# The plain down projection of a feed-forward block's first pair, placed behind the first two products of its second pair

## The chip, the cores and the metric

The kernel runs on one core of one Trainium2 chip. The metric is the device time of one execution in microseconds (us); the kernel before took 2893.24 us, the median of three runs.

## The reference: what is computed

Two layers are applied with the same weights to 256 prompt tokens and 512 sample tokens, 768 rows of width 1024, all in 32-bit floats.

```python
def swiglu_ffn(x, w_gate, w_up, w_down):
    return (jax.nn.silu(x @ w_gate) * (x @ w_up)) @ w_down
...
        for l in range(DEPTH):                     # 2 layers
            x = layer_norm(ALPHA * x + 0.5 * swiglu_ffn(x, ffn1_w_gate[l], ...), ln1_g[l], ln1_b[l])
            mix = hybrid_mixer(x, w_in[l], ...)    # neighbourhood attention and a bidirectional SSD
            x = layer_norm(ALPHA * x + mix, ln2_g[l], ln2_b[l])
            x = layer_norm(ALPHA * x + 0.5 * swiglu_ffn(x, ffn2_w_gate[l], ...), ln3_g[l], ln3_b[l])
```

The hidden width is 2816. So there are four feed-forward blocks, two in each layer. They are called block 1 to block 4 here, in order of time; between blocks 1 and 2, and between 3 and 4, lies a mixer.

## The kernel before

**Number format.** Every matmul operand is kept as a high and a low part (`XH`, `XL`; a weight tile `w` holds both). One 128-row slice of a matrix product is three matmuls: high by high, high by low, low by high. Making a weight's two parts ("splitting" it) is a copy on ACT (L106) and a subtraction on DVE (L107), or for some of them two ACT instructions and an accumulating DMA that GpSimd issues (L102 to L104).

**One block.** The hidden width is cut into 11 pairs of 256 columns. Pair 0 is plain (`plain_pair`, L408): gate and up products of all 768 tokens over all of the width, in two halves m=0 and m=1 of 128 hidden columns each, then `silu` on ACT (L461) and the product on DVE (L465). `put_h` (L435, L437) then splits the result into four tiles: h0 and h1 hold the first 384 tokens of m=0 and m=1, and h2 and h3 the last 384 tokens. Pairs 1 to 10 (`fast_pair`) use Strassen's scheme in Winograd's form: seven products instead of eight for m=0 (gate) and seven for m=1 (up), each of 12 matmuls of 384 columns (L525). Their order is `0, 1, S2, S1, S3, 3, S4`. The products `0` and `1` read `XH` and `XL` as they are. `S2`, `S3` and `3` read the sums of x called T2, T3 and T4, and `S1` reads T1, which overwrites a part of `XH` and `XL`. `sums_of_x` makes these sums once for each block, behind pair 0, on DVE (L507 to L516, L497), GpSimd (L505, L506, L508) and ACT (L496). Products whose name begins with S also need a sum of weights, which DVE makes (L90) before it is split.

**The plain down projection.** `down(0, 1)` multiplies h0 to h3 with the four down weight tiles of pair 0 and adds half of the result to `y`: for each of six token tiles t it takes two PSUM banks (tags B and C, two buffers each), issues 12 matmuls of 512 columns (L619) that alternate between them, and then evicts both with two DVE instructions (L628). In its middle (t == 2) it splits four more weights. The down projections of later pairs are run in pieces between the products of the pair behind them.

**What sets the order.** The program is written in the order pair 0, sums of x, `down(0, 1)`, pair 1 and so on. A scheduler then gives every engine its own list, mostly by that order and by what it takes to be ready first; an engine runs its list strictly in order, and waits at an instruction whose inputs are not there. The raw weights come through a ring of four tiles (`wraw`), loaded on SP's queue; split product weights go through a ring of five places, w0 to w4 (shown as `w_89` to `w_93`), and the down weights of a pair through w5 to w11 (`w_94` to `w_100`).

Of the kernel before, what the change touches and what calls it, by code (L numbers as in the profile page):

```python
# [11 lines left out]
ALU = mybir.AluOpType  # L12
# [3 lines left out]
P = 128  # L16
# [5 lines left out]
NT = T // P  # L22
# [125 lines left out]
def trunk(ctx, tc, x_in, w_gu, w_dn, w_xbc, w_z, w_qk, w_v, w_out, ln_gb, ln_gbc, conv_wb, gmix, smalls, bias, y_out):  # L148
# [265 lines left out]
    def ffn(l, w, i_ln, pend, emit_out, late=()):  # L414
# [113 lines left out]
        def fast_pair(p):  # L528
# [15 lines left out]
                    v_.tensor_mul(sg[:, i, h], sg[:, i, h], src)  # L544

            units_ = down_units(p - 1) if p - 1 in dnw else []
            half = dn_half.get((l, w, p))
            for i, (m, what) in enumerate(PRODUCTS):
                x, b, first = {0: ("B11", 1, True), 1: ("B21", 2, True), "S2": ("T2", 1, False), "S1": ("T1", 3, True),
# [12 lines left out]
                if (m, 3) in banks and (m, "S3") in saved and (m, "d") not in saved:  # L562
                    block(m, 1, hb, saved[m, "S3"], banks[m, 3])
                    saved[m, "d"] = True
                if i >= 1:
                    for _ in range(min(1 if i == 1 else 2, len(units_))):
                        units_.pop(0)()
# [15 lines left out]
        def down_units(p):  # L583
# [18 lines left out]
                    out.append(run)  # L602
            return out

        def down(a, b):
            last = b == NPAIR
            nf = 2 * (b - a)
            units = ws.get(2 * nf)
            post = []
            for t in range(NT):  # L610
                ps = (bank("B"), bank("C"))
                cols = slice(t % 3 * P, (t % 3 + 1) * P)
                for i in range(nf):
                    if i == RESTAT and len(post) > 1:
                        post.pop(0)()
                    hh, hl = (x[:, cols] for x in hs[4 * ((a + i // 2) % 2) + 2 * (t // 3) + i % 2])
                    for wi, (hx, wx) in enumerate(((hh, 0), (hh, 1), (hl, 0))):
                        for n in range(2):
                            t_.matmul(ps[n], hx, units[2 * i + n][wx], start=(i == 0 and wi == 0),  # L619
                                      stop=(i == nf - 1 and wi == 2))  # L620
                if last:
                    post.append(emit_out(t, ps))
                    if t == 2:
                        ws.split(ws.nget + 3)
                    continue
                for n in range(2):
                    sl = y[:, t, n * 512 : (n + 1) * 512]
                    v_.scalar_tensor_tensor(sl, ps[n], 0.5, sl, op0=ALU.mult, op1=ALU.add)  # L628
                if t == 2:
                    ws.split(ws.nget + 3)  # L630
            return post

        plain_pair(0)
        sums_of_x()
        down(0, 1)
        for p in range(1, NPAIR):
            fast_pair(p)
        tp.close()
# [604 lines left out]
```

## Time and profile before

| | us |
|---|---|
| median of three runs | 2893.24 |
| the three runs | 2893.24, 2877.48, 2894.02 |
| the profiled execution | 2896.72 |
| its span, first to last instruction | 2894.8 |
| PE busy / DVE busy / ACT busy in the span | 2837.5 / 2210.1 / 1580.4 |
| mean granted TensorE clock, as a share of 2.4 GHz | 0.988 |

A row of the profile's timeline gives the start of an instruction or of a merged run of them, how long it took, engine, line, operation, output and inputs, the shape, and in brackets how long the engine had been idle before it and what ended that. Matmuls are pipelined: one of 512 columns is listed with 0.39 us, but in a dense stretch the next one starts 0.23 us later. So the distance between starts is what counts.

### The profile page before, as it was taken

Reading aid. Unit: us, or ns where it says so; the run is one execution under the profiler, and the core shown is the slowest. Engines: PE = TensorE matmul, PEld = TensorE weight load, DVE = VectorE, ACT = ScalarE, POOL = GpSimd, SP = SyncE. Lnnn points to the kernel's source line nnn. Section 1 sums busy time; section 2 is a strip of 40 time slices with the busy share of each in tenths; the row PEclk is TensorE's granted clock in tenths of the full one; section 3 lists DMA queues with packets and bytes.
Section 4 is the critical chain, followed back from the end, with each engine's and each line's share of the span. In section 5 each row is a group of like instructions: output and inputs, shape, how many; then the busy total and the mean of one; then the engine's idle time right before and its main releaser. Section 6 shows DMA issues by size and latency. Waiting matters only on the chain.

```text
span 2894.8 us, 41895 instructions
## 1 busy us (share of the span) xinstructions
PE 2837.5 (98%) x15094; PEld 2521.1 (87%) x15094; DVE 2210.1 (76%) x4207; ACT 1580.4 (55%) x3231; POOL 408.5 (14%) x513
## 2 busy tenths in 40 slices
PE   8999999999999999999989999999999999999998
PEld 7999999888777899999879999989886778999997
DVE  7788887768545888888788888877673458888887
ACT  4556564657455456554645555455654564565643
POOL 2112120100001212121131112100000002121210
PEclk9999999999999999999999999999997999999999
DMA  3465563224323255564216565533233232555642
GB/s 119 117 139 127 128 146 103 103 87 142 124 81 130 70 128 129 126 146 95 95 43 139 121 136 128 127 110 122 88 111 116 76 126 71 131 127 128 145 96 88
DMA packets 128880, 330.26 MB, mean 114 GB/s; under 512 B 14816, under 2 KB 27296, under 8 KB 127904
## 3 DMA queue, kind: packets, MB, share of 16 engines
q1 hardware_dynamic: 82592, 243.68, 26.6%
q0 software_dynamic: 46080, 83.91, 16.8%
q8 instruction: 118, 1.93, 0.3%
q14 instruction: 90, 0.74, 0.1%
HBM read 224.67 MB, written 18.97 MB: 84 GB/s over the span
## 4 chain that ended last, share of the span: by engine, by line
PE 86%; DVE 6%; ACT 3%; DMA 2%; issue 2%; POOL 1%; DVEq 0%; SPq 0%; POOLq 0%; ACTq 0%
PE psA L525 37%; PE psB L597 9%; PE psC L597 7%; PE psA L408 5%; PE psA L1120 5%; PE psA L966 5%; PE psB L619 3%; PE psC L619 3%; PE psB L1055 3%; PE psA L773 2%; PE psA L993 2%; PE psC L1084 2%; DMA wraw<-in_w_dn_dram 1%; PE psB L1073 1%; DVE w L107 1%
## 5 line engine op out<-in xcount | busy, mean ns | idle before, releaser
L525 PE MATMUL psA<-XH,w 128*128 128x384 f32 x2560 | 695.9, 338 | 5.0 <-DMA w<-wraw 5.0
L525 PEld LDWEIGHTS psA<-XH,w 128*128 128x128 f32 x2560 | 467.7, 188 | 13.7 <-DMA w<-wraw 6.3
L104 POOL DMA_DIRECT2D w<-wraw x320 | 273.8, 904 | 1246.3 <-ACT w L103 1165.6
L525 PE MATMUL psA<-XL,w 128*128 128x384 f32 x1280 | 432.3, 338 | 0.0
L106 ACT CAST w<-arena 128x512 fp32r<-128x512 f32 x320 | 198.3, 620 | 236.6 <-DVE arena L90 132.9
L600 DVE SCALAR_TENSOR_TENSOR arena<-psB,arena 128x512 f32<-128x512 f32 x384 | 260.4, 685 | 63.6 <-PE psB L597 62.1
L106 ACT CAST w<-wraw 128x512 fp32r<-128x512 f32 (+1 forms) x320 | 193.9, 620 | 161.2 <-PE psA L525 69.4
L102 ACT CAST w<-wraw 128x512 fp32r<-128x512 f32 x320 | 195.2, 619 | 139.6 <-PE psA L525 64.3
L107 DVE TENSOR_TENSOR w<-wraw,w 128x512 fp32r<-128x512 f32 (+1 forms) x320 | 216.3, 687 | 65.4 <-ACT w L106 59.8
L107 DVE TENSOR_TENSOR w<-arena,w 128x512 fp32r<-128x512 f32 x320 | 216.2, 684 | 40.7 <-ACT w L106 40.1
L525 PEld LDWEIGHTS psA<-XL,w 128*128 128x128 f32 x1280 | 240.4, 188 | 7.4
L408 PE MATMUL psA<-XH,w 128*128 128x256 f32 (+1 forms) x1056 | 240.6, 334 | 5.0 <-DVE XH L373 5.0
L540 DVE TENSOR_TENSOR arena<-arena,psA 128x384 f32<-128x384 f32 x240 | 132.4, 551 | 103.9 <-ACT arena L535 85.0
L103 ACT ACTIVATE w<-w 128x512 fp32r<-128x512 f32 x320 | 195.9, 629 | 3.9
L600 DVE SCALAR_TENSOR_TENSOR arena<-psC,arena 128x512 f32<-128x512 f32 x288 | 191.6, 683 | 7.7
L408 PEld LDWEIGHTS psA<-XH,w 128*128 128x128 f32 x1056 | 167.9, 188 | 27.0 <-DVE XH L373 6.3
L525 PE MATMUL psA<-T4h,w 128*128 128x384 f32 x640 | 185.7, 351 | 3.5 <-ACT arena L535 3.0
L525 PE MATMUL psA<-T3h,w 128*128 128x384 f32 x640 | 177.0, 337 | 0.8 <-ACT arena L535 0.8
L525 PE MATMUL psA<-T2h,w 128*128 128x384 f32 x640 | 177.5, 338 | 0.0
L331 POOL TENSOR_TENSOR stat<-stat,cst 128x1 f32<-128x1 f32 x60 | 25.5, 425 | 1013.1 <-ACT arena L934 415.6
L535 ACT COPY arena<-psA 128x384 f32<-128x384 f32 x240 | 113.4, 473 | 82.5 <-PE psA L525 82.5
L408 PE MATMUL psA<-XL,w 128*128 128x256 f32 (+1 forms) x528 | 150.7, 334 | 2.0 <-DVE XL L374 2.0
(359 smaller groups left out, 6306.5 us busy)
## 6 DMA issues: line engine op xcount, KB each, us to landing
wraw<-in_w_gu_dram SPq DMA_DIRECT2D x176, 512.0 KB, 3.9
w<-wraw POOLq DMA_DIRECT2D x320, 256.0 KB, 4.2
wraw<-in_w_dn_dram SPq DMA_DIRECT2D x88, 512.0 KB, 5.2
e<-ac_d SPq DMA_DIRECT2D x48, 256.0 KB, 3.4
wraw<-in_w_xbc_dram SPq DMA_DIRECT2D x16, 512.0 KB, 4.4
wraw<-in_w_qk_dram SPq DMA_DIRECT2D x16, 512.0 KB, 3.9
arena<-in_bias_dram SPq DMA_DIRECT2D x64, 128.0 KB, 2.0
wraw<-in_w_out_dram SPq DMA_DIRECT2D x16, 512.0 KB, 4.1
```

Source lines behind the costliest of these rows:

```text
L102: nc.scalar.copy(hi, raw)
L103: nc.scalar.activation(lo, hi.bitcast(F32), AF.Copy, scale=-1.0)
L104: nc.gpsimd.dma_start(lo, raw, accum_op=ALU.add)
L106: nc.scalar.copy(hi, raw)
L107: nc.vector.tensor_sub(lo, raw, hi.bitcast(F32))
L408: t_.matmul(ps[:, o : o + b - a], w[:, k % 4], xx[:, k, a:b], start=(k == 0 and part == 0 and i == 0), stop=(k == KD - 1 and part == 1))
L525: t_.matmul(ps, wx[:, k], xx[:, k], start=first and k == 0 and i == 0, stop=k == 3 and i == 2, skip_group_check=not first)
L597: t_.matmul(ps, hx, wx, start=first and k == 0, stop=k == 2, skip_group_check=not first)
L600: v_.scalar_tensor_tensor(sl, ps, 0.5, sl, op0=ALU.mult, op1=ALU.add)
L619: t_.matmul(ps[n], hx, units[2 * i + n][wx], start=(i == 0 and wi == 0), stop=(i == nf - 1 and wi == 2))
L966: t_.matmul(ps[r][:, : b - a], w[:, k % 4], xx[:, k, a:b], start=(k == 0 and part == 0 and i == 0), stop=(k == KD - 1 and part == 1))
L1120: t_.matmul(p[n], xx[:, k, cols], wo[2 * k + n][wx], start=(i == 0 and wi == 0), stop=(i == KD - 1 and wi == 2))
```

## The change

The call `down(0, 1)` is gone. `plain_units` makes the same plain down projection as twelve pieces, one for each token tile and each half of the output columns: six matmuls into one bank, then its eviction. All twelve are issued in pair 1 behind the product `1` of m=0, so behind the first two products. `down` is left for the last two pairs alone. The splitting of four more weights in the middle of `down(0, 1)` is gone as well; the products of pair 1 ask for their weights themselves.

```diff
@@ -544,6 +544,7 @@
             units_ = down_units(p - 1) if p - 1 in dnw else []
+            after = plain_units(0, ws.get(4)) if p == 1 else []
             half = dn_half.get((l, w, p))
...
@@ -562,6 +563,9 @@
                     block(m, 1, hb, saved[m, "S3"], banks[m, 3])
                     saved[m, "d"] = True
+                if i == 1:
+                    for unit in after:
+                        unit()
                 if i >= 1:
                     for _ in range(min(1 if i == 1 else 2, len(units_))):
@@ -602,8 +606,24 @@
+        def plain_units(p, units):
+
+            out = []
+            for t in range(NT):
+                for n in range(2):
+                    def run(t=t, n=n):
+                        ps = bank("BC"[n])
+                        for i in range(2):
+                            hh, hl = (x[:, t % 3 * P : (t % 3 + 1) * P] for x in hs[4 * (p % 2) + 2 * (t // 3) + i])
+                            for k, (hx, wi) in enumerate(((hh, 0), (hh, 1), (hl, 0))):
+                                t_.matmul(ps, hx, units[2 * i + n][wi], start=i == 0 and k == 0, stop=i == 1 and k == 2)
+                        sl = y[:, t, n * 512 : (n + 1) * 512]
+                        v_.scalar_tensor_tensor(sl, ps, 0.5, sl, op0=ALU.mult, op1=ALU.add)
+
+                    out.append(run)
+            return out
+
         def down(a, b):
-            last = b == NPAIR
             nf = 2 * (b - a)
...
-                if last:
-                    post.append(emit_out(t, ps))
-                    if t == 2:
-                        ws.split(ws.nget + 3)
-                    continue
-                for n in range(2):
-                    sl = y[:, t, n * 512 : (n + 1) * 512]
-                    v_.scalar_tensor_tensor(sl, ps[n], 0.5, sl, op0=ALU.mult, op1=ALU.add)
+                post.append(emit_out(t, ps))
                 if t == 2:
                     ws.split(ws.nget + 3)
...
         plain_pair(0)
         sums_of_x()
-        down(0, 1)
```

Once line numbers and buffer numbers are left out, the lists of the two programs differ in the four blocks' starts alone, on PE in some 75 rows each, on DVE in 15 to 17, on ACT in 14 or 15; SP's list is the same. Three places are shown, all of block 1. The others have the same shape.

PE, from the last matmul of pair 0 on, before. `w_94` to `w_97` are the four down weights, `w_93` and `w_89` the weights of the products `0` and `1`, `w_90` that of `S2`, `w_91` that of `S1`, `w_92` that of `S3`.

```order
L408 MATMUL psA<-XH,w_92 128x256
L619 MATMUL psB<-w_94,h0h 128x512
...
L619 MATMUL psB<-w_96,h1h 128x512
...
L619 MATMUL psC<-w_97,h3l 128x512
...
L525 MATMUL psA<-XH,w_89 128x384
...
L525 MATMUL psA<-T2h,w_90 128x384
...
L525 MATMUL psA<-XH,w_91 128x384
...
L525 MATMUL psA<-T3h,w_92 128x384
```

The same place with the change:

```order
L408 MATMUL psA<-XH,w_92 128x256
L525 MATMUL psA<-XH,w_93 128x384
...
L525 MATMUL psA<-XH,w_89 128x384
...
L619 MATMUL psB<-w_94,h0h 128x512 x2
L619 MATMUL psB<-w_94,h0l 128x512
L619 MATMUL psB<-w_96,h1h 128x512 x2
...
L525 MATMUL psA<-T2h,w_90 128x384
...
L525 MATMUL psA<-XH,w_91 128x384
L619 MATMUL psB<-w_94,h0h 128x512 x2
...
L525 MATMUL psA<-XL,w_91 128x384
...
L525 MATMUL psA<-T3h,w_92 128x384
```

The two products (24 matmuls) now stand ahead of all down matmuls. Of the twelve pieces four (24 matmuls) stand ahead of `S2`; then come `S2`, the first matmul of `S1`, the other eight pieces (48 matmuls) and the other eleven matmuls of `S1`. Before, the whole down projection stood ahead of the products, with only a few matmuls of the product `0` among it.

DVE behind the last T2 subtraction, before:

```order
L497 TENSOR_TENSOR T2l<-arena,T2h 128x384
L516 TENSOR_TENSOR arena<-arena 128x384
L628 SCALAR_TENSOR_TENSOR arena<-psB,arena 128x512
L497 TENSOR_TENSOR T4l<-arena,T4h 128x384
L628 SCALAR_TENSOR_TENSOR arena<-psC,arena 128x512
```

The same place with the change (an eviction is L621 there):

```order
L497 TENSOR_TENSOR T2l<-arena,T2h 128x384
L516 TENSOR_TENSOR arena<-arena 128x384
L90 TENSOR_TENSOR arena<-arena,wraw 128x512
L107 TENSOR_TENSOR w_91<-arena,w_91 128x512
L497 TENSOR_TENSOR T4l<-arena,T4h 128x384
L107 TENSOR_TENSOR w_90<-arena,w_90 128x512
L90 TENSOR_TENSOR arena<-wraw 128x512
L107 TENSOR_TENSOR w_93<-wraw,w_93 128x512
L540 TENSOR_TENSOR arena<-arena,psA 128x384
L107 TENSOR_TENSOR w_92<-arena,w_92 128x512
L90 TENSOR_TENSOR arena<-wraw 128x512
L621 SCALAR_TENSOR_TENSOR arena<-psB,arena 128x512
```

The weight sums and splits of `S2`, `S1`, `S3` and `3` now stand ahead of the first eviction; before they stood between the evictions and behind them. All rows of DVE ahead of this place are unchanged, and so are the rows of ACT up to the casts of h1 and h3. In blocks 2 and 3 one more L90 stands in this stretch, since there it is not done earlier.

ACT with the change, at the first down weight of pair 1 (`w_94`):

```order
L535 COPY arena<-psA 128x384
L102 CAST w_98<-wraw 128x512
L103 ACTIVATE w_98<-w_98 128x512
L106 CAST w_94<-wraw 128x512
L102 CAST w_95<-wraw 128x512
L103 ACTIVATE w_95<-w_95 128x512
L106 CAST w_96<-wraw 128x512
L106 CAST w_91<-wraw 128x512
L102 CAST w_99<-wraw 128x512
L103 ACTIVATE w_99<-w_99 128x512
L102 CAST w_97<-wraw 128x512
L535 COPY arena<-psA 128x384
```

The cast into `w_94` must wait until the plain down projection has read its old content for the last time, and eight instructions stand between it and the copy (L535) that saves the bank behind `S3`. Before, that copy stood behind six such instructions, and the plain projection was over when they came.

## Rows read from the trace of the kernel before

**Rows 1.** The page: busy time, share of the span and instructions of each engine.

```profile
PE 2837.5 (98%) x15094; PEld 2521.1 (87%) x15094; DVE 2210.1 (76%) x4207; ACT 1580.4 (55%) x3231; POOL 408.5 (14%) x513
```

**Rows 2.** Waits of PE: who waited for whom, total us, times, longest.

```profile
PE psB L619 <- ACT h1h L435: 19.7, 4, 7.5
PE psA L525 <- DMA w<-wraw: 5.0, 4, 1.6
PE psA L525 <- ACT arena L535: 3.8, 5, 1.2
```

**Rows 3.** Stretches by block, from the first down matmul to the first T3 matmul.

```profile
core 0: us, PE busy (x) PEld busy (x) DVE busy (x) ACT busy (x) POOL busy (x), PEclk, DMA share, GB/s
49.70:81.84 32.14, 27.79 (x122) 23.74 (x121) 25.27 (x46) 10.10 (x20) 0.07 (x1) 0.89 0.10 33
964.20:995.05 30.85, 26.90 (x122) 23.10 (x121) 25.26 (x47) 10.26 (x20) 0.00 (x0) 0.94 0.12 35
1477.70:1512.87 35.17, 27.71 (x123) 23.66 (x121) 28.82 (x49) 10.36 (x21) 3.20 (x3) 0.85 0.09 30
2412.98:2443.73 30.75, 26.82 (x123) 23.00 (x121) 24.82 (x46) 10.21 (x20) 0.00 (x0) 0.94 0.11 32
```

**Rows 4.** Timeline of PE in block 1.

```profile
56.30 0.79 PE L619 MATMUL psB<-w,h1h 128*128 128x512 f32 x1 [4.35 <-ACT h1h L435]
56.90 0.63 PE L619 MATMUL psC<-w,h1h 128*128 128x512 f32 x1
...
61.16 0.63 PE L619 MATMUL psB<-w,h1h 128*128 128x512 f32 x1
...
66.36 0.40 PE L619 MATMUL psB<-w,h2h 128*128 128x512 f32 x1
...
74.65 0.34 PE L525 MATMUL psA<-XL,w 128*128 128x384 f32 x1
...
79.73 0.34 PE L525 MATMUL psA<-XH,w 128*128 128x384 f32 x1
...
81.84 0.34 PE L525 MATMUL psA<-T3h,w 128*128 128x384 f32 x1
```

**Rows 5.** Timeline of PE in blocks 2, 3 and 4: the same wait.

```profile
969.77 0.79 PE L619 MATMUL psB<-w,h1h 128*128 128x512 f32 x1 [3.95 <-ACT h1h L435]
1486.73 0.79 PE L619 MATMUL psB<-w,h1h 128*128 128x512 f32 x1 [7.46 <-ACT h1h L435]
2419.14 0.50 PE L619 MATMUL psB<-w,h1h 128*128 128x512 f32 x1 [3.93 <-ACT h1h L435]
```

**Rows 6.** Timeline of DVE in block 1.

```profile
40.37 0.67 DVE L107 TENSOR_TENSOR w<-wraw,w 128x512 fp32r<-128x512 f32 x1
...
59.14 0.54 DVE L497 TENSOR_TENSOR T2l<-arena,T2h 128x384 fp32r<-128x384 f32 x1
59.61 0.54 DVE L516 TENSOR_TENSOR arena<-arena 128x384 f32<-128x384 f32 x1
...
75.22 0.68 DVE L628 SCALAR_TENSOR_TENSOR arena<-psC,arena 128x512 f32<-128x512 f32 x1
75.82 0.68 DVE L90 TENSOR_TENSOR arena<-wraw 128x512 f32<-128x512 f32 x1
```

**Rows 7.** Timeline of DVE in blocks 2, 3 and 4: the last T2 subtraction.

```profile
972.71 0.55 DVE L497 TENSOR_TENSOR T2l<-arena,T2h 128x384 fp32r<-128x384 f32 x1
1489.67 0.54 DVE L497 TENSOR_TENSOR T2l<-arena,T2h 128x384 fp32r<-128x384 f32 x1
2422.07 0.55 DVE L497 TENSOR_TENSOR T2l<-arena,T2h 128x384 fp32r<-128x384 f32 x1
```

**Rows 8.** Stretches of the two mixers' attention, columns as in Rows 3.

```profile
771.93:921.71 149.78, 148.04 (x764) 105.89 (x764) 71.41 (x241) 82.34 (x224) 9.69 (x23) 1.00 0.33 104
2200.51:2370.47 169.96, 168.22 (x765) 118.14 (x765) 71.47 (x241) 82.74 (x224) 9.69 (x23) 0.87 0.29 92
```

**Rows 9.** The page's groups by cost: busy us, mean ns of one | idle before.

```profile
L106 ACT CAST w<-wraw 128x512 fp32r<-128x512 f32 (+1 forms) x320 | 193.9, 620 | 161.2 <-PE psA L525 69.4
```

## The prediction

> **What bounds the kernel now.** I read the engines' busy times first. PE is busy for 98% of the span [rows 1], so time can come only from what PE spends waiting or at a low clock, or be lost by adding to that. The list of PE's waits names the largest: 19.7 us in four waits, one in each block, where the down matmuls of the plain pair want h1, the half of the hidden values that comes last [rows 2]. Then I cut out the stretch of each block in which the change moves anything, from its first down matmul to its first T3 matmul. The four stretches take 128.91 us together [rows 3]. The timeline gives what their work needs at full speed: 36 down matmuls start between 66.36 and 74.65, so one every 0.230 us, and the 12 matmuls of a product take 2.11 us, 0.176 each [rows 4]. A stretch has 72 down and 48 product matmuls, 16.6 + 8.4 = 25.0 us, so four need 100.0. **28.9 us, 1.0% of the profiled execution, is all that can be won in them.** Of it 19.7 is waiting. Most of the rest is clock: behind the wait of block 1 the starts from 56.90 to 61.16 are ten steps of 0.426 us [rows 4], half pace, which is the 1.2 GHz level; the granted clock of the stretches is 0.89, 0.94, 0.85 and 0.94 [rows 3].
>
> **What is moved, step by step.** The two products now stand ahead of the down projection. Their split weights are there: the later one is done on DVE at 40.37 + 0.67, over 8 us ahead of the place [rows 6]. They read parts of x that the sums don't overwrite. So 24 x 0.176 = 4.2 us of work go where PE waited. But the first piece needs h1 after three matmuls, where the old list had more that need h0 alone. So PE comes to h1 at 4.2 + 3 x 0.23 = 4.9 us behind the stretch's start: 54.6, 969.1, 1482.6 and 2417.9. The time at which h1 is there is set by DVE and ACT, whose lists are the same up to it: 56.30, 969.77, 1486.73 and 2419.14 [rows 4, 5]. The wait shrinks from 19.7 to 1.7 + 0.7 + 4.1 + 1.2 = 7.7 us. If nothing else were late, the change would win 12 us of waiting and most of the clock's loss.
>
> But something else is late. Behind h1 stand 21 down matmuls (4.8 us), then the product S2, whose weight is a sum that DVE makes and splits only behind the last T2 subtraction; then, behind one matmul of S1, the fifth piece, which needs the bank of the first piece back, so the first eviction. That eviction now stands on DVE behind eleven instructions (twelve in blocks 2 and 3), counted from the T2 subtraction: four of 384 columns, the rest of 512. DVE starts one of 384 columns every 0.47 us and one of 512 every 0.60 [rows 6]. So for block 1 the eviction starts at 59.14 + 4 x 0.47 + 7 x 0.60 = 65.22 and ends 0.68 later, at 65.90. PE would be there sooner: S2's low weight is split at 62.43 (five instructions behind 59.14, and its own 0.68), its ten matmuls that need it and the one of S1 take 1.9, so PE arrives at 64.4 and waits 1.5 us. **DVE's list, not PE's work, then sets the end of the stretch.** From there PE has 48 down matmuls and 11 of S1, 11.0 + 1.9 = 13.0 us, to the first T3 matmul:
> block 1: 65.90 + 13.0 = 78.9, before 81.84, gain 2.9;
> block 2: 972.71 [rows 7] + 1.88 + 8 x 0.60 + 0.68 + 13.0 = 993.1, before 995.05, gain 2.0;
> block 3: 1489.67 + 7.36 + 13.0 = 1510.0, before 1512.87, gain 2.9;
> block 4: 2422.07 + 6.76 + 13.0 = 2441.8, before 2443.73, gain 1.9.
> The sum is 9.7 us. In block 3 PE still waits 4 us for h1 and its clock will fall as it did, but what that costs lies under the same wait for DVE.
>
> The number of down matmuls and of evictions stays the same; an eviction per six matmuls instead of two per twelve costs nothing, because DVE needs 0.60 for one and PE 1.38 us for six matmuls. SP's list is the same. The four weights that were split in the middle of the old down projection are now split ahead of the evictions: that is counted in the eleven. Their raw tiles come free some 10 us sooner and the next down weights are loaded sooner, into a stretch with DMA shares of 0.09 to 0.12 [rows 3], so at no cost.
>
> Left open is the clock in the new waits: 1.3 us at S2 and 1.5 at the fifth piece in block 1, up to 2.9 at S2 in blocks 2 and 3, where three more instructions stand ahead of its split. One fall ahead of the eight pieces costs at least ten steps of 0.426 - 0.230, so 2.0 us. The bounds are no fall (0) and one in each block (8). I take one fall in all, 2.0, nearer to none: the falls at these places stand behind waits of 3.9 us or more [rows 3 to 5], and the new waits are shorter; but the clock of the second attention stretch [rows 8] fell with no wait ahead that is among the long ones [rows 2], so I don't take zero. Gain: 9.7 - 2.0 = 7.7 us.
>
> The Trainium skill speaks against the change here: its page "TensorE: Matmul & The Clock Gate", section "A second HAM failure mode: psum-queue depth-cycling", tells of a kernel whose PE idles for moments between groups of matmuls that cycle through PSUM banks, and whose clock keeps changing level for it. The pieces are such groups. By that rule the time would be that of the second rival below; the trace so far shows falls only behind long waits.
>
> **The number.** The profiled execution took 2896.72 us; 7.7 less is 2889.0. It lies 3.5 above the median of the runs, 2893.24. Against the median: 2893.24 - 7.7 = **2885.5 us**. Own range of this case: from gain 1.7 (four falls) to 14 (none, and half of the 8.8 us of later waits for DMA and ACT [rows 2] gone too): 2879 to 2892. Chance 0.47.
>
> **Rivals.**
> *The clock of an attention stretch decides (0.34).* The same stretch takes 149.78 us in the first layer at full clock and 169.96 in the second at 0.87, with the same work [rows 8]: 20.2 us. One of the three runs, 2877.48, is 16 faster than the others, which fits a run without that fall. Whether it comes again is not in the change's hands, but the stretches move in time. With no fall in either layer: 2885.5 - 20.2 = 2865.3 (chance 0.27). With one in both: 2905.7 (0.07).
> *The clock stays low through the eight pieces, slower (0.06).* Place: from the fifth piece on, behind two waits close together. Price: 0.196 us for each of 48 matmuls in four blocks, 37.6 at most, so 2921; with half of them 18.8 - 9.7 = 9 above before, 2902. It decides from 12.4 matmuls in each block, where 4 x 12.4 x 0.196 eats the 9.7. For it: the new waits come in twos. Against: in block 1 dense down matmuls brought the clock back between 61.16 and 66.36 [rows 4], so within 10 us of the wait's end.
> *The gain is given back on ACT (0.13).* The cast into the first down place now waits for the last pieces, and behind it stand w_91's new content, which waits for S1's end, three more, and the copy behind S3. Price: 4 x 0.62 us [rows 9] = 2.5 a block behind S1, against S3's 2.1 us and five matmuls of m=1 (0.9) that PE has meanwhile. So it costs nothing by 0.5 us; where down weights or the subtractions on DVE come later, up to 2.5 a block, 10 in all, and the time stays at 2889 to 2895.
>
> **Range and chances.** 2863 to 2895 leaves out the lower end of the case without any fall (0.05), the case of two (0.07) and most of the slower rival (0.05). About 1% is what a measurement of this kernel can tell from no change: below 2864.3 is faster, above 2922.2 slower. Faster needs the case without any fall and a gain above 8.7: 0.11. Slower needs a clock that is low nearly throughout: 0.02. Within 1%: 0.87.
>
> **What would show it.** Right: two products at the start of each stretch with no wait; h1 waits near 1.7, 0.7, 4.1 and 1.2 us; new waits at S2 for a weight and at the fifth piece for DVE; first T3 matmuls 2 to 3 us earlier from each stretch's start; the rest of the timeline only shifted. Wrong: evictions that start well before 65.9 (counted from the same start), so a gain near 20; a copy behind S3 that PE waits for; low pace in the pieces; or a total moved by an attention stretch alone.

## The result and the profile after

The changed kernel took 2863.82 us (median of 20 runs, 2860.96 to 2887.75), the kernel before 2894.01 (20 runs, 2874.47 to 2919.71). The ratio is 0.9936, its 95% interval 0.9906 to 0.9965; it is taken of the means, without the one run of before that lies over 1.5% above its fastest. So it is faster, by 0.64%, within the 1% that had the chance of 0.87. The ratio of the medians is 0.9896: the time lies 0.8 us above the low edge of the range, and just below the 2864.3 that the prediction named as the line to "faster".

The runs don't scatter around a median. They lie in groups some 19 us apart. Before: 8 runs near 2877, 8 near 2895, 4 from 2913 to 2920. With the change: 11 near 2862, 9 near 2882, none higher. Like beside like, **the change wins 13 to 14 us; the 30 between the medians hold one step of the groups as well**, which the last part of this section is about.

With the change, the page's busy time of each engine, and then PE's waits (who waited for whom, total us, times, longest):

```profile
PE 2839.5 (98%) x15094; PEld 2517.7 (87%) x15094; DVE 2209.7 (77%) x4207; ACT 1585.1 (55%) x3231; POOL 408.8 (14%) x513
```

```profile
PE psB L619 <- ACT h1h L435: 7.1, 4, 4.0
...
PE psB L619 <- DVE arena L621: 2.6, 2, 1.3
PE psA L525 <- ACT arena L535: 2.5, 4, 0.9
...
PE psA L525 <- DMA w<-wraw: 2.3, 4, 0.9
...
PE psA L525 <- DVE w L107: 1.9, 4, 0.5
PE psA L525 <- ACT w L106: 1.7, 2, 1.5
```

Against [rows 2] the h1 waits are down from 19.7 to 7.1 us, three new kinds of 6.2 us have come (L621, L107, L106), and the later waits for DMA and for ACT's copy are down from 8.8 to 4.8, which the prediction's number had left out.

The four stretches with the change, from the first product to the first T3 matmul (columns as in [rows 3]):

```profile
49.63:79.08 29.45, 26.18 (x122) 21.62 (x121) 26.52 (x49) 13.22 (x25) 2.02 (x3) 1.00 0.16 45
985.09:1014.11 29.02, 26.37 (x122) 21.59 (x121) 26.09 (x49) 13.42 (x25) 1.73 (x2) 1.00 0.18 47
1496.09:1528.59 32.50, 27.76 (x123) 22.65 (x121) 29.57 (x51) 13.42 (x25) 4.93 (x5) 0.95 0.14 41
2407.57:2436.59 29.02, 26.23 (x122) 21.59 (x121) 26.09 (x49) 13.35 (x25) 1.73 (x2) 1.00 0.16 46
```

Together 119.99 us against 128.91 [rows 3]: 8.9 won. The granted clock holds in three of them. ACT does 25 instructions where it did 20, and GpSimd does two to five where three of four had none or one: work that came behind the stretch has moved into it.

PE in block 1 with the change: the first product, the first matmul with h1, S2's low weight, the fifth piece, T3:

```profile
49.63 0.34 PE L525 MATMUL psA<-XH,w 128*128 128x384 f32 x1
...
56.30 0.73 PE L619 MATMUL psB<-w,h1h 128*128 128x512 f32 x2 [1.57 <-ACT h1h L435]
...
62.48 0.61 PE L525 MATMUL psA<-T2h,w 128*128 128x384 f32 x2 [0.40 <-DVE w L107]
...
65.96 0.74 PE L619 MATMUL psB<-w,h0h 128*128 128x512 f32 x2 [1.30 <-DVE arena L621]
...
79.08 0.34 PE L525 MATMUL psA<-T3h,w 128*128 128x384 f32 x1
```

DVE at the same place: the last T2 subtraction, the sum for S3 (its last input is a raw gate tile), the first eviction:

```profile
59.14 0.55 DVE L497 TENSOR_TENSOR T2l<-arena,T2h 128x384 fp32r<-128x384 f32 x1
...
62.35 0.68 DVE L90 TENSOR_TENSOR arena<-wraw 128x512 f32<-128x512 f32 x1
...
65.23 0.68 DVE L621 SCALAR_TENSOR_TENSOR arena<-psB,arena 128x512 f32<-128x512 f32 x1
```

Blocks 2 to 4, PE's wait for h1, and in block 2 the wait for S2's weight:

```profile
990.64 0.73 PE L619 MATMUL psB<-w,h1h 128*128 128x512 f32 x2 [0.49 <-ACT h1h L435]
...
997.58 0.44 PE L525 MATMUL psA<-T2h,w 128*128 128x384 f32 x1 [1.55 <-ACT w L106]
...
1505.12 0.93 PE L619 MATMUL psB<-w,h1h 128*128 128x512 f32 x2 [3.98 <-ACT h1h L435]
...
2413.73 0.73 PE L619 MATMUL psB<-w,h1h 128*128 128x512 f32 x2 [1.10 <-ACT h1h L435]
```

**The other half of the gain lies behind the stretches.** In block 1, before and then with the change, PE at the next two late places and at the start of the block's last T3 product:

```profile
97.95 0.44 PE L525 MATMUL psA<-T3h,w 128*128 128x384 f32 x1 [0.82 <-ACT arena L535]
...
102.48 0.61 PE L525 MATMUL psA<-XH,w 128*128 128x384 f32 x2 [1.64 <-DMA w<-wraw]
...
486.37 0.34 PE L525 MATMUL psA<-T3h,w 128*128 128x384 f32 x1
```

```profile
97.12 0.62 PE L525 MATMUL psA<-XH,w 128*128 128x384 f32 x2 [0.47 <-DMA w<-wraw]
...
480.66 0.34 PE L525 MATMUL psA<-T3h,w 128*128 128x384 f32 x1
```

The weight that PE waited for at 102.48 is there 5.4 us sooner. Why shows on SP's queue: the first load of down weights for pair 1, before and then with the change:

```profile
76.58 2.31 SPq L72 DMA_DIRECT2D wraw<-in_w_dn_dram  x2
```

```profile
63.10 2.59 SPq L72 DMA_DIRECT2D wraw<-in_w_dn_dram  x2
```

It starts 0.75 us behind the start of the sum for S3, the last reader of the raw tile that it overwrites: 75.82 [rows 6] and 76.58 before, 62.35 and 63.10 now. The same holds in the other blocks: counted from the end of pair 0, that load starts at 26.9, 25.0, 29.4 and 25.5 us before, and at 13.5, 13.1, 16.5 and 13.1 with the change. ACT's casts of those weights then no longer stand in one crowd with those for the products. The first of them, before and then with the change:

```profile
82.65 0.62 ACT L102 CAST w<-wraw 128x512 fp32r<-128x512 f32 x1 [0.17 <-DMA wraw<-in_w_dn_dram]
```

```profile
69.61 0.62 ACT L102 CAST w<-wraw 128x512 fp32r<-128x512 f32 x1 [2.70 <-DMA wraw<-in_w_dn_dram]
```

Before, ACT is idle for at most 0.55 us at a time from 78.57 to 89.7 us.

Counted from the end of pair 0 to the last T3 matmul, the blocks won 5.6, 2.5, 3.7 and 3.4 us, 15.2 in all: 8.9 up to the first T3 matmul and 6.3 behind it.

### The attention stretch

The same stretches as in [rows 8], with the change:

```profile
766.25:942.55 176.30, 174.57 (x764) 122.18 (x764) 71.52 (x241) 82.79 (x224) 9.73 (x23) 0.84 0.28 88
2215.24:2364.99 149.75, 148.06 (x764) 105.90 (x764) 71.37 (x241) 82.38 (x224) 9.73 (x23) 1.00 0.32 104
```

Now the first layer has the low clock, for 26.5 us more; before it was the second, for 20.2. So the two profiled executions differ by 15.2 - 26.5 + 20.2 = 8.9 us, near the 9.0 by which their times differ (2896.72 and 2887.75). Five profiles of such kernels have one such stretch, and their runs lie in the middle group; that of experiment 3 has both, and lies in the highest. No profile of the kernel before or of the changed kernel caught a run of the lowest group; that it has none is read from the granted clock of the whole run, 0.997 to 0.999 there against 0.989 to 0.992 for the changed kernel. At the start of the stretch stand six groups of transposes, L1033 here, from 763.30 us on, with two waits of 1.0 us among them; the first is this one:

```profile
766.25 0.63 PE L1033 MATMUL psB<-ident,xs 128*128 128x128 f32 x4 [1.04 <-DVE XL L1039]
```

Here the clock falls: it is 0.66 from 765 to 775 us, 0.50 from 775 to 825 and 1.00 from 830 on. In the other layer it stays up behind the same waits.

### The profile page after: what moved, and what is told of

It reads as the page before. It is cut to its first block, busy times and chain, and to the rows that moved or that the text cites. A ratio compares the mean times of both kernels' runs of the same rounds, so it can differ in the third digit from the quotient of the medians.

```text
span 2885.7 us, 41893 instructions
## 1 busy us (share of the span) xinstructions
PE 2839.5 (98%) x15094; PEld 2517.7 (87%) x15094; DVE 2209.7 (77%) x4207; ACT 1585.1 (55%) x3231; POOL 408.8 (14%) x513
## 3 DMA queue, kind: packets, MB, share of 16 engines
q1 hardware_dynamic: 82592, 243.68, 26.5%
## 4 chain that ended last, share of the span: by engine, by line
PE 57%; DVE 6%; ACT 1%; issue 1%; DMA 1%; POOL 1%; DVEq 0%; POOLq 0%; ACTq 0%; SPq 0%
PE psA L525 28%; PE psB L601 7%; PE psC L601 5%; PE psA L978 2%; PE psA L408 2%; PE psA L1132 2%; PE psA L785 1%; PE psB L639 1%; PE psC L639 1%; PE psB L1067 1%; PE psA L1005 1%; DVE w L107 1%; PE psC L1096 1%; PE psB L619 1%; PE psC L619 1%
## 5 line engine op out<-in xcount | busy, mean ns | idle before, releaser
L106 ACT CAST w<-arena 128x512 fp32r<-128x512 f32 x320 | 198.3, 620 | 222.5 <-DVE arena L90 121.2
L106 ACT CAST w<-wraw 128x512 fp32r<-128x512 f32 (+1 forms) x320 | 194.1, 620 | 143.5 <-PE psA L408 38.1
L107 DVE TENSOR_TENSOR w<-wraw,w 128x512 fp32r<-128x512 f32 (+1 forms) x320 | 216.6, 687 | 65.2 <-ACT w L106 59.7
L107 DVE TENSOR_TENSOR w<-arena,w 128x512 fp32r<-128x512 f32 x320 | 216.3, 684 | 35.4 <-ACT w L106 34.9
L535 ACT COPY arena<-psA 128x384 f32<-128x384 f32 x240 | 113.6, 473 | 86.0 <-PE psA L525 86.0
```

The costliest lines, as they stand in the source:

```text
L106: nc.scalar.copy(hi, raw)
L107: nc.vector.tensor_sub(lo, raw, hi.bitcast(F32))
L535: s_.copy(t, banks[m, 1])
```

## The experiments

**1. The form without the placement.**

```diff
-            after = plain_units(0, ws.get(4)) if p == 1 else []
+            after = []
...
         sums_of_x()
+        for unit in plain_units(0, ws.get(4)):
+            unit()
```

> The twelve pieces of six matmuls, but at the old place, behind the sums of x and ahead of the two products; no split of four weights in the middle. It does the form of the change without its placement. Theory (two products as cover for h1 make the gain, and the weight sums ahead of the evictions on DVE bring the rest later in the block): h1 is waited for as before, 4 to 7 us in each block and 19 to 20 us in all, with low clock behind it; the stretches from the end of pair 0 to the first T3 matmul stay at 32.1, 30.8, 35.2 and 30.8 us within 0.7 (with the change 29.4, 29.0, 32.5, 29.0); behind them at most 2 us are won in all. Time within 3 us of before, like runs beside like. Rival 1 (the form itself, an eviction per six matmuls and no split in the middle, makes the gain): stretches near 29 to 30 us and a time like the changed kernel's, 13 to 15 us below before. Rival 2 (the gain behind the stretches comes from the dropped split): stretches as before, but 5 to 6 us less behind them.

Median 2894.68 us (10 runs; 1 at 2876, 5 near 2893, 4 from 2912 to 2922), ratio 1.0021 (0.9981 to 1.0061); group by group between 1 us more and 4 less than before. The h1 waits sum to 19.2 us. The stretches are 30.7, 30.9, 34.1 and 32.0: three miss the 0.7, both ways, and their sum, 127.7, is within 1.2 of that of before. Behind them the profile is 4.4 us shorter, 3.5 of it in block 1, more than forecast and less than the second rival's 5 to 6. The first load of down weights starts at 70.25 us here, between the 76.58 of before and the 63.10 of the change. The form alone wins little, and the first rival is out; some of the gain behind the stretches comes with the form.

**2. The placement without the form.** `plain_units` is replaced by six units of twelve matmuls that alternate between two banks, as in the old `down`.

> The old form (twelve matmuls that alternate between two banks, then two evictions) at the new place, behind two products. Six matmuls that need h0 alone now stand ahead of h1, where the pieces have three. Theory (DVE's list, not PE's cover, sets the end of the stretch): the h1 waits shrink by 0.7 us each, from 1.57, 0.49, 3.98, 1.10 to 0.9, 0, 3.3 and 0.4, but the wait for the first eviction or for the weight of S2 grows by as much, so the first T3 matmul comes 29.4, 29.0, 32.5 and 29.0 us behind the end of pair 0, within 0.3 of the changed kernel, and the time is the changed kernel's within 2 us. Rival (PE's cover sets it): each stretch 0.5 to 0.7 us shorter, 2.6 in all.

One run, 2881.63 us, where the changed kernel's runs with one slow attention stretch have 2882. PE's waits:

```profile
PE psA L525 <- ACT w L106: 5.0, 4, 2.5
...
PE psB L636 <- ACT h1h L435: 4.5, 3, 3.3
```

The h1 waits fell from 7.1 to 4.5 as forecast, and the wait for S2's weight took their place: 29.4, 30.0, 32.5 and 29.0 us. Block 2 missed by 1.0, with its clock at 0.94, as it was in the changed kernel's second profile (30.3 us). In this one profile more cover wins nothing.

**3. All of h0 first.**

```diff
+            for tt in ((0, 1), (2,), (3,), (4,), (5,)):
+                    ps = {(t, n): bank("BC"[n]) for t in tt for n in range(2)}
+                    for i in range(2):                 # h0 (h2), then h1 (h3)
+                        for t in tt:
+                            for n in range(2):
```

> At the new place, but the first four pieces do all their twelve matmuls with h0 first, in four banks, and then the twelve with h1. Theory (DVE's list sets the end): h1 is no longer waited for in blocks 1, 2 and 4, and about 1.9 us in block 3 (3.98 less 9 x 0.23), 5 us less in all; S2's weight and the first eviction come when they came, so the first T3 matmuls stay at 29.4, 29.0, 32.5 and 29.0 us within 0.4 and the time within 2 us of the changed kernel's. Rival (PE's cover sets it): stretches 1.1, 0.5, 2.1 and 1.1 us shorter or more where the clock's fall in block 3 goes too, 5 to 6 us in all, and a time near 2857 where the changed kernel has 2862.

PE's waits for S2's weight and for h1:

```profile
PE psA L525 <- ACT w L106: 8.2, 4, 2.6
...
PE psB L620 <- ACT h1h L435: 1.9, 1, 1.9
```

The h1 waits went to the 1.9 us expected, and the stretches did not get shorter: 29.5, 30.1, 33.2 and 29.4, 122.2 in sum, against 120.0 and 121.5 in two profiles of the changed kernel. The runs (2865 and 2866; 2884 to 2894; five at 2901 to 2902) are 3 to 4 us slower than the changed kernel's where no attention stretch is slow, so the time missed its 2 us, away from the rival. **5 us of waiting were taken away and nothing was won: DVE's list sets the end.** The first eviction of block 1 and the piece that needs its bank show it:

```profile
65.64 0.67 DVE L623 SCALAR_TENSOR_TENSOR arena<-psB,arena 128x512 f32<-128x512 f32 x1
...
66.36 0.73 PE L620 MATMUL psB<-w,h0h 128*128 128x512 f32 x2
```

Counted from the end of pair 0, the first eviction ends within 0.02 us of where it ends in the changed kernel, in all four blocks, and PE goes on with it in blocks 1 and 4. In blocks 2 and 3 it goes on 1.2 and 0.85 us later, with the granted clock at 0.94 and 0.90 behind longer waits for S2's weight: there the low clock took a part of what the cover could have won.

**4. The transposes among dense matmuls.** Those of the first four token tiles move in among the last matmuls of the V projection:

```diff
-        for _ in pj:
-            pass
-        for c in range(NT):
+        def to_xt(c):
...
+        for n, _ in enumerate(pj):
+            if 1 <= n <= 4:
+                to_xt(n - 1)
+        for c in range(4, NT):
+            to_xt(c)
```

> The changed kernel, with the transposes of the mixer's result for the first four token tiles moved in among the last dense matmuls of the V projection, so that the start of the attention stretch has no 5 us of transposes with two waits of 1.0 us. Theory (the run-to-run steps of 19 us come from the clock's fall at that place, after transposes and waits): the two waits go in both layers (4.1 us), the attention stretches stay at full clock, and all runs lie in one group near 2858 (2855 to 2861), without the group 19 us above; so the median is 4 to 5 below the changed kernel's fast group and 25 to 37 below before. Rival 1 (the fall comes from the attention's own sparse matmuls, wherever the transposes stand): still a third or more of the runs 18 to 20 us above the others. Rival 2 (the waits only move behind, to the scores of the attention): less than 2 us won in runs without a fall.

6 runs, 2856.89 to 2860.29 us, median 2859.33: one group, as forecast, 3.0 below the changed kernel's lowest (4 to 5 forecast). The transposes overwrite rows that a token tile of the V projection still read, so some of its sums are taken over other data; its instructions are the same. Experiment 6 puts them one tile later.

**5. The changed kernel again.**

> The changed kernel once more, beside the kernel before. Its runs should again fall into groups near 2862, 2882 and perhaps 2901 us, by none, one or two attention stretches at a low clock, each group 13 to 15 us below the same group of before (2877, 2896, 2915). Theory (the change wins 14 us in the blocks and does not govern the attention stretch): the share of runs without a fall is as in the runs of before, about 0.2 to 0.6. Rival (the change itself makes the fall rarer): half or more of the runs without a fall and none with two, as in its first 20 runs, and before again with two falls in some.

7 runs near 2862, 5 near 2880 (12 runs, ratio 0.9935, 0.9903 to 0.9967). Before, beside it: 10 near 2875, 18 near 2895, 1 at 2914. The groups lie 13 and 15 us apart, like beside like. The 7 of 12 without a fall fit both the theory and the rival. Counted by the groups, the kernel before had the slow clock in 70 of 180 attention stretches over all runs (31 runs of 90 without), the changed kernel in 14 of 64 (18 of 32 without), experiments 1 and 3 in 13 of 20 each. So its share differs from kernel to kernel by more than chance makes likely, and not with the gain: experiment 3 has the changed placement and twice the share of before. What sets it stays open.

**6 and 7. The change with quiet attention.** The edit of experiment 4, a tile later, on the changed kernel and on the kernel before (the V projection's generator yields its tile number `t`):

```diff
+        late = iter(((0, 1), (2,), (3,), ()))
+        for t in pj:
+            if t is not None and t >= 4:
+                for c in next(late):
+                    to_xt(c)
```

> The changed kernel with the transposes of tiles 0 to 3 among the last 36 matmuls of the V projection, each behind the projection of the rows that it overwrites (in the run before this one they stood a token tile too early). Theory (the fall starts at the transposes and the two waits of 1 us behind them): one group of runs, 2857 to 2861 us, none 18 us above it; attention stretches 2 to 2.5 us shorter each than an undisturbed one. Rival (the attention's own sparse matmuls): a third or more of the runs 18 to 20 us higher.

> The kernel before with the same transposes among the V projection. With the attention out of the way, what the change does in the blocks stands alone. Theory (gain in the blocks 13 to 15 us, 8.8 of it up to the first T3 matmul and the rest behind): one group near 2872 (2870 to 2875), 13 to 15 us above the changed kernel with the same edit. Rival (part of the gain came from the attention stretches): less than 10 us above it; as predicted before the run (7.7 us in the blocks): 2866 to 2868.

Changed kernel: 2855.28 to 2856.30 us (4 runs, median 2855.72, ratio to before 0.9892, 0.9843 to 0.9941). Kernel before: 2869.27 to 2871.28 (10 runs, median 2870.49). Each is one group, **14.8 us apart**, on the same chip. That is what the change is worth by itself, and the 7.7 of the prediction is out. The two profiled executions differ by 13.0; in them the stretches are 5.9 us shorter (121.0 against 126.9) and what lies behind them 6.2, so some 1 us of it, and the rest up to 14.8, is put down to no row. The changed kernel came 1 us below its forecast of 2857 to 2861, the kernel before lies in its 2870 to 2875 (two of ten runs just below). From the first matmul of the V projection to the last of the attention it is 183.7 us in both layers, against 186.3 without the edit where the clock holds. In experiments 4, 6 to 10 and 12, 44 runs, no run lies 18 us above the others. So the fall hangs on the transposes that stand in a row with waits, and not on the attention's own matmuls alone. The row and the waits are not told apart. PE's waits of the kernel before with this edit, for comparison below:

```profile
PE psB L619 <- ACT h1h L435: 19.2, 4, 7.5
...
PE psA L525 <- DMA w<-wraw: 5.0, 4, 1.6
...
PE psA L525 <- ACT arena L535: 4.6, 8, 1.2
```

**8. Evictions first, on experiment 6:** cover without the early weights. The scheduler also moves S2 on PE with this edit: it stands behind all twelve pieces.

```diff
-                product(ws.get(1, NGU - 1)[0], x, banks[m, b], first)
+                product(ws.get(1, 2 if p == 1 and i < 2 else NGU - 1)[0], x, banks[m, b], first)
```

> On the changed kernel with the transposes among the V projection: for the first two products of pair 1 weights are split only two ahead, so that on DVE the first eviction stands behind seven instructions, not eleven, and the weight sums and splits of S3 and 3 stand behind the evictions. Theory: the first eviction comes 2.3 us sooner and the wait at the fifth piece (1.3 us in blocks 1 and 4) goes, so the first T3 matmul comes 1 to 1.4 us sooner in blocks 1 and 4 and unchanged within 0.4 in 2 and 3, where S2's weight sets the time; but the raw gate weights come free some 10 us later, the down weights of pair 1 with them, and of the 6.3 us won behind the stretches 3 to 6 are lost: 1 to 4 us slower than the kernel without this edit. Rival 1 (the gain behind the stretches has nothing to do with when the raw tiles come free): 2 to 3 us faster. Rival 2 (the first eviction does not set the end): stretches unchanged within 0.3 in all four blocks.

2872.15 us (10 runs, 2869.86 to 2878.18): **16 us slower, the whole gain gone.** DVE's first eviction and its sum for S3, then SP's first load of down weights, then two of PE's waits:

```profile
63.10 0.68 DVE L621 SCALAR_TENSOR_TENSOR arena<-psB,arena 128x512 f32<-128x512 f32 x1
...
77.37 0.68 DVE L90 TENSOR_TENSOR arena<-wraw 128x512 f32<-128x512 f32 x1
...
78.12 2.30 SPq L72 DMA_DIRECT2D wraw<-in_w_dn_dram  x2
```

```profile
PE psA L525 <- ACT arena L535: 5.9, 8, 1.2
PE psA L525 <- DMA w<-wraw: 5.6, 4, 1.4
```

Again 0.75 us from the sum to the load, but 15 later. The stretches are 119.2 us in sum, 1.9 shorter than experiment 6's, and what lies behind them 15.6 longer (from the same profiles, to the last T3 matmul). PE's waits behind the stretches sum to 15.3 us against 4.3 there, so 11 of the 16 us are such waits; the rest is put down to no row. The direction was forecast, 1 to 4 us in size; the size was wrong by far. The stretches missed their forecast too: that of block 1 is 1.0 us longer, that of block 2 is 2.0 shorter. Experiment 10 has S2 behind all pieces as well, with the early weights, and loses nothing behind the stretches; so S2's new place is not what costs here.

**9. The early weights without the cover,** on experiment 7.

```diff
             units = ws.get(2 * nf)
+            if not last:
+                ws.split(ws.nget + 4)
             post = []
...
-                if t == 2:
-                    ws.split(ws.nget + 3)
```

> On the kernel before with the transposes among the V projection (2870.5 us): five weights (0, 1, S2, S1, S3) are asked for at the start of the old down projection, none in its middle. It does the order of the weights on DVE without the cover: the down projection still starts ahead of the products, so h1 is waited for as before (19 us in four waits, low clock behind them), but the first eviction now stands on DVE behind weight sums and splits, six instructions of which stood behind evictions before; PE has most of the two products between the second and the third token tile, so no bank is waited for long. Theory (the change has two halves: cover wins the stretches, the early weight sums win what is behind them, since gate weights come free and down weights are loaded some 10 us sooner): first T3 matmuls within 1 us of the kernel without this edit in each block (30.7, 30.7, 35.0, 30.6), the first down load of pair 1 near 63 to 66 us in place of 75.9, 4 to 8 us won behind the stretches: 2862 to 2867 us. Rival 1 (the cover alone brings both): no gain, 2869 to 2872. Rival 2 (the order of the weights alone brings it all): 2855 to 2859.

SP's first load of down weights in block 1, and PE's waits:

```profile
63.14 8.51 SPq L72 DMA_DIRECT2D wraw<-in_w_dn_dram  x2
```

```profile
PE psB L621 <- ACT h1h L435: 19.6, 4, 7.4
...
PE psA L525 <- DMA w<-wraw: 2.4, 4, 0.7
...
PE psA L525 <- ACT arena L535: 1.4, 3, 0.7
```

2865.5 us (4 runs, 2864.1 to 2866.38), 5.0 less than experiment 7, as forecast; the load comes 12.7 us sooner, the later waits shrink from 9.6 to 3.8, h1 is waited for as before. Two stretches came 1.5 us later, past the 1 that was allowed. (Experiments 9 to 12 did not run beside 6 and 7; the kernel before, which ran beside each, differs there by up to 2 us, group by group.) **Cover alone wins nothing (8 against 7: 1.7 us slower, with runs spread over 8 us), early weights alone win 5.0, both together 14.8.** PE that is ahead only runs into late weights; weights that are early help little behind an h1 that is late.

**10. Half of the cover,** on experiment 6.

```diff
-                if i == 1:
+                if i == 0:
                     for unit in after:
```

> On the changed kernel with the transposes among the V projection (2855.7 us): the pieces behind the first product, not behind the first two, so half of the cover. The h1 waits grow by about 2.1 us each, to 3.5, 2.6, 6.0 and 3.2 us. Theory (DVE's list sets the end of the stretch and the second product then stands behind the waiting pieces; only a clock fall costs): the first T3 matmul 0 to 1 us later where the clock holds, 1.5 to 2.5 later where it falls behind the longer wait; weights as early as with the change; 2857 to 2864 us. Rival (each us of cover counts): 8.4 us in all, 2864 us or more, with the low clock's cost on top.

PE's wait for h1, and SP's first load of down weights in block 1:

```profile
PE psB L619 <- ACT h1h L435: 15.5, 4, 6.1
```

```profile
63.20 8.72 SPq L72 DMA_DIRECT2D wraw<-in_w_dn_dram  x2
```

2859.56 us (4 runs, 2858.11 to 2860.78): the h1 waits are 8.6 us longer than experiment 6's 6.9, and 3.8 are lost, as forecast. But PE's order changed too: S2 stands behind all pieces, and no wait for its weight is left and almost none for an eviction. The stretches are 31.6, 29.3, 33.1 and 29.1 us, 123.2 in sum against 121.0, with the granted clock at 0.89, 0.94, 0.90 and 1.00. So 8.6 us of waiting cost 2.2 there, because the waits behind them went. Behind the stretches nothing is lost (0.1 us), and the two profiled executions differ by 2.5.

**11. One wait less at the transposes.**

```diff
-            ps = bank("BC"[c % 2])
+            ps = bank("BCBCAA"[c])
```

> The changed kernel with its six groups of transposes where they were, in one row ahead of the attention, but in six banks of their own, so that the first of the two waits (1.04 us for a bank) goes and the second (1.01 us for XH) stays. Theory A (the fall needs both waits close together): no run 18 us above the others, and 2 us less than the changed kernel in its fast group, so one group near 2860. Theory B (transposes and one wait are enough): 2 to 5 of 10 runs 18 to 20 us above the others.

4 runs, 2858.0 to 2860.78, none 18 us higher. It is not decisive: the changed kernel has 18 of 32 runs without a fall, so four in a row come about once in ten. Of the 3.5 us won against its lowest group 2.8 are the waits: in each layer the first is gone and the second is 0.64 us instead of 1.01.

**12. One weight later,** on experiment 6: an attempt at a better version.

```diff
-                product(ws.get(1, NGU - 1)[0], x, banks[m, b], first)
+                product(ws.get(1, NGU - 2 if p == 1 and i == 1 else NGU - 1)[0], x, banks[m, b], first)
```

> On the changed kernel with the transposes among the V projection (2855.7 us): behind the second product weights are split three ahead instead of four, so that only the weight of product 3 comes behind the first evictions; the sums for S2, S1 and S3 stay ahead. On DVE the first eviction stands behind eight instructions, not eleven. Theory (the first eviction's place sets the end of the stretch, and what is behind it hangs on the sums of S3, which free a raw tile): the wait of 1.3 us at the fifth piece in blocks 1 and 4 goes, first T3 matmuls 0.5 to 1.5 us sooner in two or more blocks; the first down load stays near 63 us and the second comes some 6 us later at no cost; 2852 to 2855 us. Rival 1 (any raw tile that comes free later costs, as in the run with the evictions first): 2857 to 2865. Rival 2 (PE finds another wait at the same place): 2855 to 2857.

PE at the fifth piece of block 1:

```profile
64.41 0.72 PE L619 MATMUL psB<-w,h0h 128*128 128x512 f32 x2 [2.08 <-DVE arena L621]
```

2858.52 us (6 runs, 2858.04 to 2859.92), no gain. The first eviction came sooner, but the scheduler then put the fifth piece ahead of most of S2, and PE waited 2.08 us for it instead of 1.30. The stretches sum to 121.3 us against 121.0: the second rival's case, though the time lies in the first's 2857 to 2865. Experiment 6 stays the best version: 39 us below before by medians, some 20 below runs of before without a fall.

## Why the prediction came out as it did

- **The h1 waits.** Forecast 1.7, 0.7, 4.1 and 1.2 us; they are 1.57, 0.49, 3.98 and 1.10. Right.
- **DVE's list sets the end.** The first eviction was placed at 65.22 and starts at 65.23; the fifth piece at 65.90 starts at 65.96; first T3 matmul 79.08, forecast 78.9. The gains 2.9, 2.0, 2.9 and 1.9 came out 2.7, 1.8, 2.7 and 1.7. In all four blocks the fifth piece starts 0.05 or 0.06 us behind the end of the first eviction; in blocks 2 and 3 PE has waited for S2's weight just before, so that almost no wait is left there. In block 2:

```profile
1000.26 0.68 DVE L621 SCALAR_TENSOR_TENSOR arena<-psB,arena 128x512 f32<-128x512 f32 x1
...
1001.00 0.73 PE L619 MATMUL psB<-w,h0h 128*128 128x512 f32 x2
```

  Experiments 2 and 3 show the cause: up to 5 us less of h1 waits don't move the first eviction, and don't bring the end forward.
- **The clock's 2.0.** The profiled run had one fall, in block 3, hidden under the wait for DVE as said, so nothing was paid. In the second profile block 2 took 30.3 us in place of 29.0, clock 0.94, from the same instructions: one visible fall costs 1.3, where 2.0 was put down. Experiments 2, 4, 6, 11 and 12 have block 2 at 30.0 to 30.5 us and 0.94 too, so one visible fall is the usual case and the first profile the exception. The 7.7 for the stretches stands beside 7.4 (second profile) and 8.9 (first).
- **The step that failed:** "the next down weights are loaded sooner, into a stretch with DMA shares of 0.09 to 0.12 [rows 3], so at no cost". That it happens was seen, and only its cost was asked for, never its gain. It is worth 6.3 us behind the stretches in the profiles; experiments 8, 9 and 10 show that the cover's gain does not last without it. The 8.8 us of later waits were in the trace [rows 2], and stood only as the upper edge of a range (half of them, gain 14). That edge was the result, 13 to 14 us by the groups and 14.8 in experiments 6 and 7.
- **The attention stretch (0.34).** "No fall in either layer", 2865.3 us with a chance of 0.27, is what the median run was, 2863.8. Where it went wrong is the frame: 2893.24 is the middle group of before, and 7.7 was taken from it as if it were the centre of one distribution. With 14 instead of 7.7 the middle group would have been forecast at 2879, and is at 2882. With 11 of 20 runs in the lowest group, one run more in the other would have moved the median by 8 us. So it is luck that the time lies near 2865.3 and not near the 2882 of the other group; the range held both, and the lower with 0.8 us to spare. The 2885.5 that the prediction named missed it by 22 us. Of these 18 are the step from the middle group to the lowest, and 4 are the larger gain.
- **Slower, the clock low through the pieces (0.06).** It did not happen. The granted clock is 1.00 in three of four stretches and 0.95 in block 3, where it fell behind h1's 3.98 us, although PE goes through groups of six matmuls in changing banks with short waits ahead. The Trainium skill's section "A second HAM failure mode: psum-queue depth-cycling", on the page "TensorE: Matmul & The Clock Gate", tells of a kernel whose clock keeps changing level at such groups; the rows of this case don't show that: in block 1 the down matmuls start 0.23 us apart from 66.54 on. The prediction's words beside it, that the trace shows falls only behind long waits, leave out the fall of [rows 8], which by its own account stands behind none.
- **The gain given back on ACT (0.13).** The opposite: product `3`, which reads T4, is not held (seven instructions stand between that cast and the copy, not eight), and the waits behind ACT's copy shrank from 3.8 to 2.5 us.

## What to carry to other kernels

When work moves between a producer and its consumers, price both sides: what the waiting engine gains, and which buffers come free sooner or later on the queues that feed it. An eviction or a sum that reads a raw tile last is the trigger of the next load, so its place in an engine's list can be worth as much as the wait that one set out to remove. Where runs fall into groups, compare group with group, or first quiet the stretch that makes them.

## What the hardware showed beside that

- At six groups of transposes in a row with two waits of 1.0 us the clock halved, in some executions and not in others of the same program. With the attention's small matmuls behind them it then stayed at 0.50 for tens of us (775 to 825 in the first profile of the changed kernel) and cost 19 to 27 us, where behind the wait of 4.35 us in block 1 dense matmuls brought it back within 10 [rows 4].
- The same waits (0.5, 1.5 and 0.5 us in block 2) left the clock at 1.00 in one profiled execution of the changed kernel and are followed by 0.94 in the other, and in experiment 6.
- SP's load into a raw tile started 0.74 to 0.76 us behind the start of the DVE sum for S3, which reads a raw tile, in every block of the eight kernels looked at (before, changed, experiments 1 and 6 to 10), while the place of that sum in block 1 moved by up to 14 us.
